# A decoder trunk on one core: the delta rule's input projections as nested block products

## The chip, the cores and the metric

The kernel runs on one core of a Trainium2 chip. The metric is the device time of one execution in microseconds (us). TensorE (PE) multiplies matrices and writes into the eight banks of PSUM; VectorE (DVE), ScalarE (ACT) and GpSimd (POOL) compute element by element; DMAs are issued here by SyncE (SP) and, a few, by POOL.

## What is computed

One layer over 1024 tokens of width 1024, all in float32. Cut to what matters:

```python
x = x + 0.5 * swiglu(rms_norm(x, ffn1_norm), gate1, up1, down1)    # width 2816
h = rms_norm(x, mix_norm)
proj = einsum("bld,de->ble", h, w_in)      # 8 delta-rule heads, 16 SSM heads, gates
q, k, v = split(silu(causal_dwconv(gdn_qkv, gdn_conv_w)))          # 4 taps, per channel
o = gated_delta_rule(q, k, v, g, beta)     # chunked recurrence, 8 heads of 128
o = rms_norm(o, gdn_norm_w) * silu(gdn_z)
y = ssd_scan(...)                          # Mamba-2 heads, gated and normalised
x = x + concat(o, y) @ w_out
x = x + 0.5 * swiglu(rms_norm(x, ffn2_norm), gate2, up2, down2)
return rms_norm(x, final_norm)
```

A delta-rule head needs four blocks of 128 columns of `w_in`: q, k, v and the output gate z (`COL_Q`, `COL_K`, `COL_V`, `COL_GZ`).

## The kernel before

**Matmuls in three.** Every large product is done on float32 operands split into a high part, rounded to the format that TensorE reads at full rate, and a low part, the remainder: high x high, high x low, low x high (`mm3`). A split is a cast on ACT and a subtraction on DVE (`wsplit` for weights, `split` elsewhere).

**Stages.** In order: the first gate and up projections (`gate_up_all`), the first down projection (`down_all`), four SSM units (`un`, four heads each), eight delta-rule heads (`h`), the out projection, and gate, up and down again. Gate, up and down are already done as 7 block products for 8: the operands are cut in 2 x 2 blocks, seven sums of blocks of each side are multiplied, and the results are combined. `prep(grp)` in `gate_up_all` makes the operands of the next product, `hid_store` writes the result to DRAM in the seven sums that the down projection reads. In the down projection `m3`, in the pool `dtmp0`, takes the first product's result (L596).

**A head.** `next_w()` gives two column blocks of `w_in`, split into `whi` and `wlo`, and loads the next ones. `proj_half` runs 8 x 3 matmuls for one block of 128 columns and one half of the tokens into a bank of the tag `pj` (three banks). `conv_silu` copies the two halves to `pre`, multiplies by the last tap, adds the other three taps with three DVE instructions over 1024 tokens (L784), and takes the silu. For z the silu goes straight from the bank (L1124). Then come the products `kt` x `kt` and `kt` x `qt` (L1149, L1150), the inverse of the 32 x 32 blocks by 31 steps of two small DVE instructions (`fx`, L1206 and L1208) with trips through DRAM (`fs_u`, `fs_x`), the merges to 128 x 128 on TensorE (L1226 to L1254), `kd` (L1265), and the recurrence over eight blocks of 128 tokens. A step of it is `kt` x state, `rr`, `u` x `rr`, `vn` (L1282), the output, and the new state `sn` (L1294).

**After the heads.** `out_start`, in the text of head 7, loads the first group of `w_out` and the SSM results into `wst`, splits them into `whi`, `wlo` and `mtt`; `group_tile` multiplies them. `nat` and `zg` are buffers of the out projection.

**Order.** The text is written stage by stage; the framework puts each engine's instructions, and each queue's DMAs, in an order of its own. It goes by readiness in its plan and prefers what stands earlier in the text, so that the projections of a later head fill TensorE between the steps of an earlier head's recurrence. On the chip each engine and each queue runs its list in that order, and each instruction waits by semaphores for its operands and for the release of the buffer that it writes. A pool opened where a closed one lay takes its memory, tile by tile.

Of the kernel before, what the change touches and what calls it, by code (L numbers as in the profile page):

```python
# [44 lines left out]
def kernel(  # L45
# [17 lines left out]
    def psum(tag):  # L63
        return ps.tile([P, 512], F32, name="ps_" + tag, tag=tag, bufs=PS_BUFS[tag])
# [8 lines left out]
    g_scr = dram.tile([NG, L], F32, name="g_scr")  # L73
    mix_scr = [dram.tile([P, NB, 256], F32, name=f"mix_scr{i}") for i in range(4)]
# [151 lines left out]
    def hsl(h, k, s):  # L226
        return h[k // 2][:, k % 2, s]
# [14 lines left out]
    def split(hi, lo, src):  # L242
        return split2(hi, lo, src)[1]
# [108 lines left out]
    def gate_up_all(pool, H, w_gate, w_up, scr, raws, ops, last, work, tail):  # L352
# [66 lines left out]
        for i, (p, w) in enumerate(todo):  # L419
# [209 lines left out]
    for h in range(GH):  # L629
        w_seq.append((COL_Q + h * P, COL_K + h * P))  # L630
        w_seq.append((COL_V + h * P, COL_GZ + h * P))
# [6 lines left out]
    def next_w():  # L638
        w = w_ready.pop(0)
        prefetch()  # L640
        return w

# [129 lines left out]

    def conv_silu(pool, w, j, cw, c, dst, bias=None, between=None):
# [9 lines left out]
        for t in range(3):  # L783
            V.scalar_tensor_tensor(out=dst, in0=pre[:, t:t + L], scalar=cw[:, t, c:c + 1], in1=dst,  # L784
                                   op0=ALU.mult, op1=ALU.add)
# [124 lines left out]

    rstd_g = []
    for un in range(4):
# [35 lines left out]
        proj_z(zts)  # L948
        xdts, xes = [], []
# [16 lines left out]
        def state():  # L966
# [3 lines left out]
            sn = s2p.tile([P, 256], F32, name="sn2", bufs=6)  # L970
# [135 lines left out]

    cn = ExitStack()
    natp = cn.enter_context(tc.tile_pool(name="natp", bufs=1, side="right", reuse_waits="tile"))
    with ExitStack() as cg:
        g1 = cg.enter_context(tc.tile_pool(name="gdn1", bufs=1, reuse_waits="tile"))  # L1110
        g2 = cg.enter_context(tc.tile_pool(name="gdn2", bufs=2, reuse_waits="tile"))
        for h in range(GH):
# [64 lines left out]
            qsq = g1.tile([P, L], F32, name="qsq")  # L1177
# [81 lines left out]
            for half in range(2):  # L1259
                pt = psum("sc")  # L1260
                for i in range(4):
                    b = half * 4 + i
                    T.transpose(pt[:, i * P:(i + 1) * P], kt[:, b * P:(b + 1) * P], ident)
                hb = slice(half * 4, half * 4 + 4)
                V.tensor_tensor(out=kd[:, hb], in0=pt.rearrange("p (i c) -> p i c", i=4),  # L1265
                                in1=wend[:, hb, h:h + 1].to_broadcast([P, 4, P]), op=ALU.mult)
# [3 lines left out]
            for b in range(NB):  # L1270
# [11 lines left out]
                V.tensor_scalar(out=vn, in0=p2[:, 0:P], scalar1=br2[:, b:b + 1], scalar2=None, op0=ALU.mult)  # L1282
# [204 lines left out]
```

## Time and profile before

| | us |
|---|---|
| median of 3 runs | 2309.29 (2308.17 to 2310.2) |
| the profiled execution | 2309.97 |
| its span in the trace | 2308.2 |
| PE busy | 2272.5 (98%) |
| DVE busy | 1725.1 (75%) |
| ACT busy | 1088.8 (47%) |
| POOL busy | 53.1 (2%) |
| DMA | 281.42 MB, mean 122 GB/s |

Busy time is the union of an engine's instructions. PE rows overlap (a matmul's printed duration is longer than its share of a run of matmuls), so distances between starts say more than durations. Issuing a DMA is not counted as busy. An idle time in a row is that of the engine just before these instructions, with what released it.

### The profile page before, as it was taken

To read this page: it belongs to the slowest core of one execution; us is meant where nothing else is said; L and a number is where in the kernel's file an instruction comes from. 1 tells how busy PE (TensorE), PEld (TensorE's weight loads), DVE (VectorE), ACT (ScalarE), POOL (GpSimd) and SP (SyncE) were. 2 spreads that over 40 slices of the span, in tenths; PEclk is the share of its full clock that TensorE was granted. 3 is DMA by queue.
4 is the path that set the end of the run, shared out by engine and by line. 5 is a ranking of instruction groups with operands and counts; after the bars stand their busy time and mean duration, and the time that the engine had idled before them with its cause. 6 is when DMAs were issued, how large, how long until landed. Compare 5 with 4: busy or idle time off the path is not lost.

```text
span 2308.2 us, 31393 instructions
## 1 busy us (share of the span) xinstructions
PE 2272.5 (98%) x11750; PEld 1858.9 (81%) x11750; DVE 1725.1 (75%) x3349; ACT 1088.8 (47%) x1884; POOL 53.1 (2%) x125
## 2 busy tenths in 40 slices
PE   7999999999999999999999999999999999999998
PEld 5788888888878888878788888788778888888886
DVE  7977776767765675668777888878688777766787
ACT  7433333343367785863555555332543333334344
POOL 0000000000000100000000000000000000000000
PEclk9999999999999999999999999999999999999999
DMA  3333332573652332232333322335223333329446
GB/s 111 127 114 102 105 109 97 178 278 128 222 179 78 92 92 81 67 85 74 83 101 83 82 74 73 104 110 193 79 84 117 109 103 105 109 88 354 139 154 214
DMA packets 231438, 281.42 MB, mean 122 GB/s; under 512 B 57449, under 2 KB 164045, under 8 KB 230261
## 3 DMA queue, kind: packets, MB, share of 16 engines
q1 hardware_dynamic: 231028, 279.31, 37.5%
q8 instruction: 92, 1.51, 0.3%
q14 instruction: 62, 0.50, 0.1%
q0 software_dynamic: 256, 0.10, 0.0%
HBM read 211.59 MB, written 67.77 MB: 121 GB/s over the span
## 4 chain that ended last, share of the span: by engine, by line
PE 87%; DVE 6%; ACT 3%; DMA 2%; issue 1%; SPq 0%; POOL 0%; DVEq 0%; ACTq 0%
PE ps_pj L121 9%; PE ps_pj L123 9%; PE ps_pj L122 9%; PE ps_pj L334 6%; PE ps_pj L332 6%; PE ps_pj L333 6%; PE ps_mx L332 3%; PE ps_mx L334 3%; PE ps_mx L333 3%; PE ps_pj L553 2%; PE ps_pj L554 2%; PE ps_pj L552 2%; PE ps_oo L333 2%; PE ps_oo L332 2%; PE ps_oo L334 2%; PE ps_sc L552 1%
## 5 line engine op out<-in xcount | busy, mean ns | idle before, releaser
L121 PE MATMUL ps_pj<-hhi,whi 128*128 128x512 f32 x832 | 334.3, 402 | 0.4 <-ACT gsb L826 0.4
L123 PE MATMUL ps_pj<-hhi,wlo 128*128 128x512 f32 x832 | 334.5, 402 | 0.0
L122 PE MATMUL ps_pj<-hlo,whi 128*128 128x512 f32 x832 | 331.8, 399 | 0.0
L334 PE MATMUL ps_pj<-bh,al 128*128 128x512 f32 x688 | 267.9, 389 | 0.0
L333 PE MATMUL ps_pj<-bl,ah 128*128 128x512 f32 x688 | 267.8, 389 | 0.0
L332 PE MATMUL ps_pj<-bh,ah 128*128 128x512 f32 x688 | 267.6, 390 | 0.0
L123 PEld LDWEIGHTS ps_pj<-hhi,wlo 128*128 128x128 f32 x832 | 156.7, 188 | 29.6 <-issue 1.9
L122 PEld LDWEIGHTS ps_pj<-hlo,whi 128*128 128x128 f32 x832 | 156.7, 188 | 29.1 <-issue 1.2
L121 PEld LDWEIGHTS ps_pj<-hhi,whi 128*128 128x128 f32 x832 | 156.8, 188 | 28.8 <-ACT gsb L826 0.9
L239 ACT CAST ah<-wst 128x512 fp32r<-128x512 f32 x88 | 54.6, 623 | 223.8 <-PE ps_oo L333 131.4
L239 ACT CAST hid<-hraw 128x1024 fp32r<-128x1024 f32 (+1 forms) x84 | 82.3, 981 | 147.9 <-PE ps_oo L554 62.5
L333 PEld LDWEIGHTS ps_pj<-bl,ah 128*128 128x128 f32 x688 | 129.2, 188 | 26.8
L334 PEld LDWEIGHTS ps_pj<-bh,al 128*128 128x128 f32 x688 | 129.1, 188 | 26.7
L332 PEld LDWEIGHTS ps_pj<-bh,ah 128*128 128x128 f32 x688 | 128.9, 188 | 26.5
L315 DVE TENSOR_TENSOR as<-wst 128x512 f32<-128x512 f32 x220 | 144.8, 683 | 3.3 <-DMA wst<-in_ffn_w_up_dram 3.1
L240 DVE TENSOR_TENSOR al<-as,ah 128x512 fp32r<-128x512 f32 x220 | 140.9, 684 | 4.8 <-ACT ah L239 4.0
L332 PE MATMUL ps_mx<-bh,ah 128*128 128x512 f32 x352 | 138.3, 395 | 4.0 <-ACT m L341 1.4
L333 PE MATMUL ps_mx<-bl,ah 128*128 128x512 f32 x352 | 138.3, 393 | 0.5 <-DVE bl L240 0.5
L334 PE MATMUL ps_mx<-bh,al 128*128 128x512 f32 x352 | 137.7, 391 | 0.3 <-DVE al L240 0.3
L239 ACT CAST ah<-as 128x512 fp32r<-128x512 f32 x220 | 125.0, 618 | 22.6 <-DVE as L315 22.6
L240 DVE TENSOR_TENSOR hid<-hraw,hid 128x1024 fp32r<-128x1024 f32 (+1 forms) x84 | 95.0, 1131 | 34.8 <-ACT hid L239 34.3
L341 ACT COPY m<-ps_pj 128x512 f32<-128x512 f32 x88 | 51.6, 588 | 124.5 <-PE ps_pj L334 122.3
(448 smaller groups left out, 5085.0 us busy)
## 6 DMA issues: line engine op xcount, KB each, us to landing
hraw<-hid_scr SPq DMA_DIRECT2D x70, 512.0 KB, 3.9
hid_scr<-hs SPq DMA_DIRECT2D x110, 256.0 KB, 2.3
wst<-in_ffn_w_down_dram SPq DMA_DIRECT2D x50, 512.0 KB, 4.7
wst<-in_ffn_w_gate_dram SPq DMA_DIRECT2D x22, 1024.0 KB, 5.6
wst<-in_ffn_w_up_dram SPq DMA_DIRECT2D x22, 1024.0 KB, 5.4
wst<-in_w_in_dram SPq DMA_DIRECT2D x36, 512.0 KB, 4.8
hid_scr<-sg SPq DMA_DIRECT2D x44, 256.0 KB, 2.0
keep<-in_ffn_w_down_dram SPq DMA_DIRECT2D x20, 512.0 KB, 5.5
```

What stands on the lines that cost most here:

```text
L121: T.matmul(o, lhsT=wh, rhs=mh, start=first, stop=False)
L122: T.matmul(o, lhsT=wh, rhs=ml, start=False, stop=False)
L123: T.matmul(o, lhsT=wl, rhs=mh, start=False, stop=last)
L239: return (A.copy(out=hi, in_=src), V.tensor_tensor(out=lo, in0=src, in1=hi.bitcast(F32), op=ALU.subtract))
L240: V.tensor_tensor(out=lo, in0=src, in1=hi.bitcast(F32), op=ALU.subtract))
L315: V.tensor_tensor(out=t, in0=v[0], in1=v[1], op=v[2])
L332: T.matmul(bank, lhsT=wh[:, k], rhs=bh[:, k], start=a, stop=False, skip_group_check=True)
L333: T.matmul(bank, lhsT=wh[:, k], rhs=bl[:, k], start=False, stop=False, skip_group_check=True)
L334: T.matmul(bank, lhsT=wl[:, k], rhs=bh[:, k], start=False, stop=z, skip_group_check=True)
L341: A.copy(out=t, in_=bank)
L552: T.matmul(bank, lhsT=hh, rhs=wh, start=first and k == 0, stop=False, skip_group_check=True)
L553: T.matmul(bank, lhsT=hh, rhs=wl, start=False, stop=False, skip_group_check=True)
```

## The change

The projections of heads 1 to 7 become block products too. For a pair of column blocks (q and k, or v and z: a *chunk*) the weights, 1024 x 256, are cut into a11, a12 (the first block's two halves of the input width) and a21, a22 (the second's); the tokens' operand into b11, b12 (first half of the width; first and second half of the tokens), b21, b22. Seven products of 512 x 128 by 512 x 512, with three matmuls per 128 rows each, take the place of eight.

- The weights' operands of all 14 chunks (a11, a12, a22 and four sums; high and low part) are made by `win_units`, a generator that `prep` advances during the first gate and up phase; what is left over is run behind that phase in the text. A unit's high part is an ACT copy; its low part is an ACT negation of the high part, to which a DMA issued by POOL adds the source; a second DMA from POOL stores both to DRAM (`wu_scr`). The pool `side0` holds a raw chunk (one buffer) and the units (two).
- The tokens' operands for products 7, 6, 5 and 4 are made in the four SSM units, one 128-row block each (`token_operands`), and stored (`t_scr`). After head 0 they are loaded into `nat` and `zg`, `whi` and `wlo`, and, for product 4, over a part of `hhi` and `hlo`.
- A head loads its 14 units through four slots in `wst`, four products ahead, and forms the results by adding in PSUM and with copies (`chunk`). The convolution reads them from SBUF in halves (`conv_from`).
- `kd` and `vn` move from DVE to ACT. `sn2` has 5 buffers for 6; `qsq` shares the buffer of `zc`.

Cut to its core:

```diff
+    IN_ORDER = (1, 6, 2, 7, 5, 3, 4)
+    def win_units(pool, tmp):
+        for c, scr in enumerate(wu_scr):
+            h = c // 2 + 1
+            raw = pool.tile([P, 2, NK, P], F32, name="wraw")
+            for j, c0 in enumerate(((COL_Q, COL_K), (COL_V, COL_GZ))[c % 2]):
+                nc.sync.dma_start(out=raw[:, j], in_=win_v[:, :, c0 + h * P:c0 + (h + 1) * P])
+            a11, a12, a21, a22 = raw[:, 0, 0:4], raw[:, 0, 4:8], raw[:, 1, 0:4], raw[:, 1, 4:8]
+            def unit(m, src):
+                u = pool.tile([P, 2, 4, P], F32R, name="wunit", bufs=2)
+                A.copy(out=u[:, 0], in_=src)
+                lo = u[:, 1].bitcast(F32)
+                A.mul(out=lo, in_=u[:, 0].bitcast(F32), mul=-1.0)
+                G.dma_start(out=lo, in_=src, accum_op=ALU.add)
+                G.dma_start(out=scr[:, IN_ORDER.index(m)].rearrange("p i (k c) -> p i k c", k=4),
+                                in_=u.bitcast(F32))
+            def summed(x, y, op):
+                t = tmp.tile([P, 4, P], F32, name="wsum", tag="m2f")
+                V.tensor_tensor(out=t, in0=x, in1=y, op=op)
+                return t
+            yield
+            unit(1, a11)
+            yield
+            unit(2, a12)
+            s1 = summed(a21, a22, ALU.add)
+            yield
...
@@ gate_up_all, prep
+                next(side, None)
@@ gate_up_phase
+            with tc.tile_pool(name=f"side{n}", bufs=1, reuse_waits="tile") as sp:
+                side = win_units(sp, npool) if n == 0 else iter(())
+                gate_up_all(npool, H, w_gate, w_up, hid_scr[n], raws, ops, last, work, [dn.prep, dn.prep], side)
+                for _ in side:
+                    pass
@@ SSM unit, behind proj_z(zts)
+        token_operands(un)
...
+    def unit_load(s):
+        if s < 7 * len(wu_scr):
+            c, i = divmod(s, 7)
+            u = slots[s % 4]
+            nc.sync.dma_start(out=u.bitcast(F32), in_=wu_scr[c][:, i])
+            units.append((s, u))
+    def unit_prod(bank, m, first):
+        s, u = units.pop(0)
+        bh, bl = H_IN[m]
+        for k in range(4):
+            wh, wl = (u[:, i, k * P:(k + 1) * P] for i in range(2))
+            T.matmul(bank, lhsT=wh, rhs=bh[k], start=first and k == 0, stop=False, skip_group_check=True)
+            T.matmul(bank, lhsT=wh, rhs=bl[k], start=False, stop=False, skip_group_check=True)
+            T.matmul(bank, lhsT=wl, rhs=bh[k], start=False, stop=k == 3, skip_group_check=True)
+        unit_load(s + 4)
+    def chunk(d0, d1):
+        lo, hi = slice(0, 512), slice(512, L)
+        x = psum("pj")
+        unit_prod(x, 1, True)
+        A.copy(out=d1[:, lo], in_=x)
+        y = psum("pj")
+        unit_prod(y, 6, True)
+        V.tensor_tensor(out=y, in0=y, in1=d1[:, lo], op=ALU.add)
+        A.copy(out=d0[:, hi], in_=y)
+        unit_prod(x, 2, False)
+        A.copy(out=d0[:, lo], in_=x)
+        unit_prod(y, 7, False)
+        z = psum("pj")
+        unit_prod(z, 5, True)
+        A.copy(out=d1[:, hi], in_=z)
+        V.tensor_tensor(out=d1[:, hi], in0=y, in1=d1[:, hi], op=ALU.add)
+        unit_prod(z, 3, False)
+        V.tensor_tensor(out=d0[:, hi], in0=z, in1=d0[:, hi], op=ALU.add)
+        unit_prod(y, 4, False)
+        A.copy(out=d1[:, lo], in_=y)
+    def conv_from(pre, c, dst):
+        for i in range(2):
+            ts = slice(i * 512, (i + 1) * 512)
+            A.mul(out=dst[:, ts], in_=pre[:, 3 + i * 512:3 + (i + 1) * 512], mul=cw_g[:, 3, c:c + 1])
+            for t in range(3):
+                V.scalar_tensor_tensor(out=dst[:, ts], in0=pre[:, t + i * 512:t + (i + 1) * 512],
+                                       scalar=cw_g[:, t, c:c + 1], in1=dst[:, ts], op0=ALU.mult, op1=ALU.add)
+        A.activation(out=dst, in_=dst, func=AF.Silu)
...
@@ heads
+            else:
+                pre = [gp.tile([P, 1028], F32, name="pre"), g1.tile([P, 1028], F32, name="pre2")]
...
+                chunk(pre[0][:, 3:3 + L], pre[1][:, 3:3 + L])
+                conv_from(pre[0], h, qt)
+                conv_from(pre[1], 8 + h, kt)
...
+                chunk(pre[:, 3:3 + L], zc)
+                conv_from(pre, 16 + h, vt_)
+                A.activation(out=zc, in_=zc, func=AF.Silu)
...
-                V.tensor_tensor(out=kd[:, hb], in0=pt.rearrange("p (i c) -> p i c", i=4),
-                                in1=wend[:, hb, h:h + 1].to_broadcast([P, 4, P]), op=ALU.mult)
+                for i in range(4):
+                    b = half * 4 + i
+                    A.mul(out=kd[:, b], in_=pt[:, i * P:(i + 1) * P], mul=wend[:, b, h:h + 1])
...
-                V.tensor_scalar(out=vn, in0=p2[:, 0:P], scalar1=br2[:, b:b + 1], scalar2=None, op0=ALU.mult)
+                A.mul(out=vn, in_=p2[:, 0:P], mul=br2[:, b:b + 1])
```

More of the change, by code (lines that the diff above doesn't have):

```diff
@@ L73 @@
     g_scr = dram.tile([NG, L], F32, name="g_scr")
+    wu_scr = [dram.tile([P, 7, 2, 512], F32, name=f"wu_scr{i}") for i in range(2 * GH - 2)]
+    t_scr = {m: dram.tile([P, 2, 4, 512], F32, name=f"t_scr{m}") for m in (4, 5, 6, 7)}
     mix_scr = [dram.tile([P, NB, 256], F32, name=f"mix_scr{i}") for i in range(4)]
@@ L628 @@
         w_seq.append((COL_SZ + un * 256, None))
-    for h in range(GH):
-        w_seq.append((COL_Q + h * P, COL_K + h * P))
-        w_seq.append((COL_V + h * P, COL_GZ + h * P))
+    w_seq.append((COL_Q, COL_K))
+    w_seq.append((COL_V, COL_GZ))
     w_ready = []
@@ L782, in conv_silu @@
             A.mul(out=dst[:, half * 512:(half + 1) * 512], in_=p, mul=cw[:, 3, c:c + 1])
-        for t in range(3):
-            V.scalar_tensor_tensor(out=dst, in0=pre[:, t:t + L], scalar=cw[:, t, c:c + 1], in1=dst,
-                                   op0=ALU.mult, op1=ALU.add)
+        conv_taps(pre, cw, c, dst)
         if bias is None:
@@ L909, in token_sums, with token_operands, put, step @@
         nc.sync.dma_start(out=dst, in_=scr.rearrange("j (c p) -> p (j c)", p=P))
+    def token_operands(k):
+        b11, b12, b21, b22 = ([hsl(t, k + 4 * i, slice(j * 512, (j + 1) * 512)).bitcast(F32) for t in (hhi, hlo)]
+                              for i in range(2) for j in range(2))
+        def put(m, t):
+            hi = tt.tile([P, 512], F32R, name="thi")
+            lo = tt.tile([P, 512], F32R, name="tlo")
+            split(hi, lo, t)
+            for i, part in enumerate((hi, lo)):
+                nc.sync.dma_start(out=t_scr[m][:, i, k], in_=part.bitcast(F32))
+        def step(t, x, y, op):
+            V.tensor_tensor(out=t, in0=x, in1=y, op=op)
+        t = tt.tile([P, 512], F32, name="tsum")
+        step(t, b22[0], b12[0], ALU.subtract)
+        step(t, t, b22[1], ALU.add)
+        step(t, t, b12[1], ALU.subtract)
+        put(7, t)
+        step(t, t, b11[0], ALU.add)
+        step(t, t, b11[1], ALU.add)
+        put(6, t)
+        step(t, b22[0], t, ALU.subtract)
+        step(t, t, b22[1], ALU.add)
+        put(5, t)
+        for x, y in ((b21[0], b22[0]), (b21[1], b22[1])):
+            step(t, t, y, ALU.subtract)
+            step(t, t, x, ALU.add)
+        put(4, t)
+    tt = cs_.enter_context(tc.tile_pool(name="tokens", bufs=1, side="right", reuse_waits="tile"))
     rstd_g = []
@@ new lines, in first_token_tiles @@
+    def first_token_tiles():
+        H_IN[7] = []
+        for i, tag in enumerate(("nat", "zg")):
+            t = natp.tile([P, 4, 512], F32R, name="t3", tag=tag)
+            nc.sync.dma_start(out=t.bitcast(F32), in_=t_scr[7][:, i])
+            H_IN[7].append([t[:, k] for k in range(4)])
+        for m in (6, 5):
+            H_IN[m] = []
+            for i, tag in enumerate(("whi", "wlo")):
+                t = wp.tile([P, 4, 512], F32R, name=f"t{m}", tag=tag)
+                nc.sync.dma_start(out=t.bitcast(F32), in_=t_scr[m][:, i])
+                H_IN[m].append([t[:, k] for k in range(4)])
+        for m, k0, j in ((1, 0, 0), (2, 4, 0), (3, 4, 1), (4, 0, 1)):
+            H_IN[m] = [[hsl(t, k0 + k, slice(j * 512, (j + 1) * 512)) for k in range(4)] for t in (hhi, hlo)]
+        for i, t in enumerate((hhi, hlo)):
+            for j in range(2):
+                nc.sync.dma_start(out=t[j][:, :, 512:L].bitcast(F32), in_=t_scr[4][:, i, 2 * j:2 * j + 2])
+        for i in range(2):
+            t = wp.tile([P, 2, 2, 512], F32R, name="wunits", tag="wst")
+            slots.extend(t[:, j] for j in range(2))
+        for s in range(4):
+            unit_load(s)
@@ L1107 @@
+    slots, H_IN = [], {}
     cn = ExitStack()
```

50 lines of the change are left out of this document (36 added, 14 removed).

## The prediction

> **What bounds the kernel now.** I read the page first (shares, chain, costliest groups), then busy time by stretch, then single stretches in order of time.
>
> ```profile
> span 2308.2 us, 31393 instructions
> PE 2272.5 (98%) x11750; PEld 1858.9 (81%) x11750; DVE 1725.1 (75%) x3349; ACT 1088.8 (47%) x1884; POOL 53.1 (2%) x125
> PE 87%; DVE 6%; ACT 3%; DMA 2%; issue 1%; SPq 0%; POOL 0%; DVEq 0%; ACTq 0%
> L121 PE MATMUL ps_pj<-hhi,whi 128*128 128x512 f32 x832 | 334.3, 402 | 0.4 <-ACT gsb L826 0.4
> ```
>
> TensorE is busy 98% of the span and carries 87% of the chain that ended last. The projections, L121 to L123, are its largest group, with no idle time before them worth the name. The kernel is bound by the number of matmuls it issues, as long as every other engine stays ahead. By stretch (us; then busy time and instructions of PE, PEld, DVE, ACT, POOL; clock, DMA share, GB/s): first gate and up phase, its beginning of the down phase, the SSM units, heads 0 to 6.
>
> ```profile
> 10.00:493.00 483.00, 475.34 (x2106) 389.30 (x2107) 371.76 (x598) 202.43 (x342) 0.00 (x0) 1.00 0.38 131
> 463.00:493.00 30.00, 30.00 (x133) 24.54 (x132) 18.11 (x18) 14.84 (x18) 0.00 (x0) 1.00 0.99 376
> 680.00:1008.00 328.00, 327.30 (x1877) 269.09 (x1876) 206.19 (x284) 243.81 (x446) 26.55 (x37) 1.00 0.29 86
> 1064.00:1437.00 373.00, 371.27 (x2543) 299.86 (x2541) 295.93 (x981) 194.37 (x391) 17.77 (x59) 1.00 0.30 78
> ...
> L1247 PE MATMUL ps_sc<-lv,u x128: 218/218/267, 1070.6 to 1518.8; 64*64 64x64 f32 x128
> ```
>
> In every stage PE leaves 1 to 2% idle. DVE and ACT have room everywhere, DVE least (0.77 to 0.79 in the first and the last of these stretches). The DMA engines are a third busy, except in one stretch where 376 GB/s is 0.99 of them: that is their ceiling here. L1247 runs once a head, so a head takes (1518.8 - 1070.6) / 7 = 64.0 us.
>
> A matmul's printed duration overlaps its neighbours. What one costs is the distance of starts in an undisturbed run:
>
> ```profile
> 1287.62 0.39 PE L121 MATMUL ps_pj<-hhi,whi 128*128 128x512 f32 x1
> ...
> 1302.12 0.39 PE L122 MATMUL ps_pj<-hlo,whi 128*128 128x512 f32 x1
> ```
>
> 64 steps lie between these two: 14.50 / 64 = 0.2266 us.
>
> **The change, part by part.** *1. Fewer matmuls.* Before, a head has 4 column blocks x 2 token halves x 8 k x 3 = 192 projection matmuls. After, it has 2 chunks x 7 products x 4 k x 3 = 168, of the same shape. Over 7 heads 168 go: 168 x 0.2266 = **-38.1 us**, on the path, since PE is the path.
>
> *2. DVE and ACT in a head.*
>
> ```profile
> L136 ACT CAST whi<-wst 128x1024 fp32r<-128x1024 f32 x64 | 65.9, 1048 | 41.7 <-PE ps_pj L122 27.7 <-PE ps_pj L123 9.5 <-DMA wst<-in_w_in_dram 4.5
> L137 DVE TENSOR_TENSOR wlo<-wst,whi 128x1024 fp32r<-128x1024 f32 x64 | 77.7, 1220 | 10.6 <-ACT whi L136 9.7
> L782 ACT ACTIVATE qt<-ps_pj,cols 128x512 f32<-128x512 f32 x16 | 11.1, 691 | 0.1
> L341 ACT COPY m<-ps_pj 128x512 f32<-128x512 f32 x88 | 51.6, 588 | 124.5 <-PE ps_pj L334 122.3 <-DVE as L315 1.2 <-ACT m L467 0.7
> L784 DVE SCALAR_TENSOR_TENSOR qt<-pre,cols,qt 128x1024 f32<-128x1024 f32 x24 | 30.7, 1280 | 6.8 <-ACT qt L782 6.6
> L461 DVE TENSOR_TENSOR m<-ps_pj,m 128x512 f32<-128x512 f32 x40 | 27.6, 690 | 4.0
> L1265 DVE TENSOR_TENSOR kd<-ps_sc,wend 128x512 f32<-128x512 f32 x16 | 10.9, 681 | 1.1 <-PE ps_sc L1263 0.7
> L1282 DVE TENSOR_SCALAR vn<-ps_sc,br 128x128 f32<-128x128 f32 x64 | 22.3, 348 | 9.4 <-PE ps_sc L1280 9.1
> L1137 ACT ACTIVATE dt<-dt,ngc 128x128 f32<-128x128 f32 x64 | 20.3, 393 | 0.1
> ```
>
> DVE loses 4 wlo, 2 kd and 8 vn (4.9 + 1.4 + 2.8 = 9.0 us). It gains 6 additions on banks (4.1) and 18 half-wide taps for 9 wide ones (18 x 0.69 against 9 x 1.28, +0.9): -4.0. ACT loses 4 whi, 6 copies, 6 multiplies and 2 silus (4 x 1.05 + 8 x 0.59 + 6 x 0.69 = 13.1). It gains 10 copies, 6 multiplies, a wide silu of two half ones' time (1.2), 8 kd and 8 vn (5.9 + 4.1 + 1.2 + 16 x 0.39 = 17.4): +4.3. At 64 us a head DVE had 50.8 and ACT 33.3. At 58.6 they have 46.8 and 37.6, so neither becomes the bound. A vn takes 0.39 for 0.35; but it now queues behind ACT's wide instructions (1.05) where it queued behind DVE's (1.28). I take nothing.
>
> *3. Waits on banks.* In a chunk the products alternate over three banks, and each copy or addition has another product (12 x 0.2266 = 2.7 us) to hide behind, but one: product 3 accumulates into z, and ACT must first have copied z after product 5. Uncovered, that is 14 x 0.59 = 8 us; the next chunk's first product and the previous head's recurrence are free to be put there. I take 2, bounds 0 and 8. A unit's load (512 KB, 4.8 us below) is issued as its slot empties and has three products, 8.2 us: hidden; without that cover it is 4.8 us a product.
>
> *4. Into the out projection.* The units hold both `wst` buffers, and the token operands `whi` and `wlo`, to the end of head 7.
>
> ```profile
> wst<-in_w_out_dram SPq DMA_DIRECT2D x8, 1024.0 KB, 5.1
> L1088 ACT ACTIVATE mtt<-nat,cols x8: 1137/1147/1152, 1433.4 to 1503.4; 128x1024 fp32r<-128x1024 f32 x8
> L121 PE MATMUL ps_pj<-whi,mtt x192: 387/389/504, 1435.3 to 1608.7; 128*128 128x512 f32 x192
> ```
>
> The first `mtt` matmul now comes at 1435.3, as the last projections end. After, the 1 MB in the second buffer can load only then: 5.1 + 1.15, and as much on DVE, are 7.5 us. Head 7's small products cover a part. +5, bounds 0 and 7.5.
>
> *5. Token operands.* Each SSM unit gets 15 DVE instructions of 512 columns (15 x 0.69 = 10.3 us), 4 ACT casts and 8 stores. DVE goes from 206 to 247 of 328 us, so this hides behind the projections that follow; but DVE is in order, and `xdt` stands behind it. +4, bounds 0 and 20 (half of each block uncovered).
>
> *6. The weight operands, in the gate and up phase.* 14 chunks of one 1 MB load, 7 units and 4 sums; a unit is an ACT copy, an ACT negation, an accumulating DMA (256 KB) and a store (512 KB), the last two issued by POOL.
>
> ```profile
> L315 DVE TENSOR_TENSOR as<-wst 128x512 f32<-128x512 f32 x220 | 144.8, 683 | 3.3 <-DMA wst<-in_ffn_w_up_dram 3.1
> L239 ACT CAST ah<-as 128x512 fp32r<-128x512 f32 x220 | 125.0, 618 | 22.6 <-DVE as L315 22.6
> hid_scr<-hs SPq DMA_DIRECT2D x110, 256.0 KB, 2.3
> x_scr<-xtb SPq DMA_DIRECT2D x8, 512.0 KB, 2.8
> wst<-in_w_in_dram SPq DMA_DIRECT2D x36, 512.0 KB, 4.8
> colst<-in_gdn_conv_w_dram POOLq DMA_DIRECT2D x1, 48.0 KB, 5.7
> colst<-in_ffn_norm_dram POOLq DMA_DIRECT2D x2, 4.0 KB, 6.4
> L596 ACT ACTIVATE m<-ps_pj x6: 584/589/598, 481.5 to 2117.8; 128x512 f32<-128x512 f32 x6
> ...
> L1066 SPq DMA_DIRECT2D zg<-z_scr x8: 319/384/578, 1008.4 to 1591.9; - x8
> ```
>
> DVE gets 56 x 0.68 = 38 us, ACT 98 x 1.24 = 122; both fit (410 and 324 of 483). The serial loop is what counts: two `wunit` buffers, one raw buffer. If both accumulations are issued ahead of the stores, two units take 1.24 + a + s, a and s being the times from issue to landing. With about 2.5 us a chunk until the next raw load is in, all is done at 12 + 35 + 98 x (1.24 + a + s) / 2. It has to be done when `m3`, which takes that memory, is written: 481.5 (L596). The program can run ahead of its text (L1066, text of the out projection, starts at 1008), so the start near 12 is open to it. This gives a + s = 7.6 us as the point from which it decides. No accumulating DMA is in the trace. The nearest in size, kind and load are the stores of 256 and 512 KB, a + s = 2.3 + 2.8 = 5.1: done at 358. The nearest from POOL, at the crowded start, give 5.7 + 6.4 = 12.1: done at 701. I take 6.8, nearer to the stores by size, for POOL's slower start: done at 441, **0 us**. Without the cover it is rival A.
>
> [...]
>
> **Sum.** -38.1 + 2 + 5 + 4 + 0 = -27. The profiled execution took 2309.97 (1.8 outside its span), 0.7 above the median, 2309.29; so 2283 either way.
>
> **Rivals.** *A, the other side: the loop of part 6 becomes the bound.* ACT and POOL are in order: a `wunit` copy that waits for a late store holds up the casts (L239) that feed PE. Beside the 131 GB/s of this stage, 14.7 MB of loads, 25.7 of accumulations and 51.4 of stores by 481.5 make 325 GB/s, against 376 at a share of 0.99; such a share lengthens every landing, and an accumulation also reads what it adds to. At a + s = 9 the loop ends at 549, 67 us late: 2283 + 67 = 2350; at 12.1, 220 late: 2503. From 7.6 on it costs, from 8.2 on it eats the 27. Against it: 5.1 from the stores.
>
> [...]
>
> *B, the change does not do what it says: a head stays at 64 us.* The recurrence of a head, the exponentials and products for the head after next, the small triangular solve on DVE and its trips through DRAM form a loop over two heads. The merges start some 2.3 us after the last row of the solve can have landed:
>
> ```profile
> lv<-fs_x SPq DMA_DIRECT2D x32, 32.0 KB, 1.9
> 1311.66 0.46 SPq L1218 DMA_DIRECT2D lv<-fs_x  x1
> 1315.92 0.21 PE L1226 MATMUL ps_sc<-lv,u 32*32 32x32 f32 x1
> ```
>
> If that loop binds, PE idles the 38 us instead, and parts 4 and 5 stay: 2309 - 0 to 8 (DVE's 4 us a head on that loop, in part) + 9 = 2310 to 2318. Against it: DVE is relieved, the wide instructions between the solve's steps are halved, and PE was never seen waiting there (1.7 us in 373).
>
> **How the numbers follow.** The forecast, 0.58, with its own range 2268 to 2300: from all covers holding (-38, and some 4 from a shorter loop) to half the bounds of parts 3 to 5. A 0.30: 2312 to 2503, most of it below 2350. B 0.12, three quarters of it within 0.2% (about what a measurement here tells from no change, 4.6 us). Faster 0.58, same 0.09, slower 0.33. The range for 8 in 10 goes from 2268 to 2345, leaving out A's far part.
>
> **What would show it.** PE matmuls 11582 for 11750, and a head at 58 to 60 us between L1247's groups, show part 1; 64 shows B. In the first phase: DMA share near 0.8 with PE still at 98%, and `m3` near 481, show part 6; PE idle released by ACT `ah`, ACT idle released by the stores of `wunit`, and a phase that ends later show A, and make the forecast wrong. PE idle ahead of the first `mtt` products sizes part 4, in front of `xdt` part 5.

## The result, and the profile after

The changed kernel takes 2524.64 us (median of 4 runs) where the kernel before takes 2309.56 in the same session: a ratio of 1.0936, 95% interval 1.0917 to 1.0955. It is 215 us slower; the forecast was 2283. Code lines of before stand 2 lines or more later after the change (L332 is L334, L341 is L343, L239 is L241, L552 is L555, L824 is L878, L1247 is L1428 and so on).

From the page after, as before: the span, the busy times, the mean granted clock and the DMA share in 40 slices, and the first line of the chain.

```profile
span 2521.6 us, 32207 instructions
PE 2314.4 (92%) x11582; PEld 1867.5 (74%) x11582; DVE 1772.4 (70%) x3462; ACT 1215.1 (48%) x2203; POOL 190.5 (8%) x321
PEclk9998988898789999999999999999999999999999
DMA  3677778789854734432655555543522332337545
PE 59%; issue 11%; DMA 10%; DVE 8%; ACT 5%; POOL 2%; POOLq 0%; SPq 0%; ACTq 0%; DVEq 0%
```

TensorE carried 87% of the chain and carries 59%. The damage is in the first third: there seven of the first twelve clock digits are below 9, and the DMA digits are mostly 7 to 9. By stretch (same columns as in the prediction):

```profile
10.00:493.00 483.00, 399.43 (x1629) 316.58 (x1629) 316.58 (x531) 226.26 (x405) 89.31 (x127) 0.91 0.71 206
493.00:600.00 107.00, 89.18 (x341) 70.10 (x342) 61.35 (x95) 45.71 (x79) 24.96 (x35) 0.89 0.84 249
600.00:725.00 125.00, 68.13 (x237) 52.08 (x236) 46.63 (x50) 47.13 (x68) 23.89 (x34) 0.74 0.84 261
725.00:880.00 155.00, 152.57 (x689) 125.69 (x688) 112.49 (x145) 67.95 (x89) 0.65 (x2) 1.00 0.54 177
1216.00:1641.00 425.00, 409.48 (x2676) 324.95 (x2675) 324.33 (x1170) 218.46 (x506) 18.80 (x62) 0.98 0.57 169
1641.00:1660.00 19.00, 13.18 (x61) 10.11 (x60) 17.16 (x62) 11.61 (x14) 1.04 (x6) 0.73 0.63 176
```

The first row had 475 us of TensorE and a clock of 1.00 before. No engine is full in it, not even the DMA engines (0.71). So something waits. The waits of the whole trace (engine, tile, line, then who ended the wait: us, times, longest), and the stores of the units (first and last start):

```profile
ACT wunit L659 <- DMA wu_scr<-wunit: 280.3, 66, 10.8
POOL wu_scr L663 <- DMA wunit<-wsum: 189.7, 48, 8.6
POOL wu_scr L663 <- DMA wunit<-wraw: 109.1, 34, 8.3
PE ps_pj L334 <- ACT m L343: 81.3, 20, 10.6
PE ps_pj L555 <- ACT m L599: 22.6, 1, 22.6
L663 POOL DMA_DIRECT2D wu_scr<-wunit x98: 547/552/880, 75.7 to 725.4; - x98
wu_scr<-wunit POOLq DMA_DIRECT2D x98, 512.0 KB, 3.9
wunit<-wsum POOLq DMA_DIRECT2D x56, 256.0 KB, 4.8
wunit<-wraw POOLq DMA_DIRECT2D x42, 256.0 KB, 4.2
```

98 units take 650 us, 6.7 each, and the first store is issued at 75.7: the first raw load is issued at 65.5 us. POOL waits for each accumulation to land before it issues the store; ACT waits for that store before it may write the buffer again; behind ACT's copy stand the copies that empty TensorE's banks (L343) and the casts of its operands (L241). The row of L599 is `m3`, which takes the units' memory: it is written at 719.8 us for 481.5 before, and TensorE waits 22.6 us for it in the down phase. ACT's timeline shows the first kind of wait (start, duration; the idle time before it, and its end, in brackets):

```profile
302.50 0.59 ACT L343 COPY m<-ps_pj 128x512 f32<-128x512 f32 x1
308.95 0.62 ACT L659 CAST wunit<-wsum 128x512 fp32r<-128x512 f32 x1 [5.86 <-DMA wu_scr<-wunit]
309.60 0.63 ACT L661 ACTIVATE wunit<-wunit 128x512 f32<-128x512 f32 x1
310.14 0.60 ACT L241 CAST ah<-wst 128x512 fp32r<-128x512 f32 x1
...
318.16 0.62 ACT L659 CAST wunit<-wraw 128x512 fp32r<-128x512 f32 x1 [3.73 <-DMA wu_scr<-wunit]
...
319.86 1.13 ACT L241 CAST ah<-as 128x512 fp32r<-128x512 f32 x2
328.29 0.62 ACT L659 CAST wunit<-wsum 128x512 fp32r<-128x512 f32 x1 [7.29 <-DMA wu_scr<-wunit]
328.94 0.63 ACT L661 ACTIVATE wunit<-wunit 128x512 f32<-128x512 f32 x1
329.47 0.57 ACT L343 COPY m<-ps_pj 128x512 f32<-128x512 f32 x1
```

The copies at 302.5 and 329.5 empty TensorE's banks; between them ACT stands three times, 5.9, 3.7 and 7.3 us, for a store that TensorE has no use for yet. Four markers cut the span into stages (first gate-weight matmul; first multiplication by the last tap in head 0, L838; last projection matmul; first `mtt` matmul):

```profile
L878 PE MATMUL ps_pj<-hhi,gw x16: 387/395/478, 878.6 to 895.7; 128*64 128x512 f32 x16
L1210 PE MATMUL ps_pj<-hhi,wunits x224: 387/393/501, 1215.9 to 1640.9; 128*128 128x512 f32 x112
L123 PE MATMUL ps_pj<-whi,mtt x192: 387/389/796, 1654.2 to 1824.3; 128*128 128x512 f32 x192
```

| stage (us) | before | after | one-chunk kernel (below) |
|---|---|---|---|
| gate, up, down | 667.5 | 878.6 (+211.1) | 669.0 |
| SSM units | 287.4 | 289.7 (+2.3) | 289.8 |
| projections of the heads | 479.4 | 473.0 (-6.4) | 471.7 |
| to the first `mtt` product | 1.0 | 12.9 (+11.9) | 12.8 |
| the rest | 872.9 | 867.4 (-5.5) | 868.8 |

Two questions follow: how the 211 come about, and where some 32 of the 38 us of saved matmuls went (38.1 less the 6.4 in the table).

### The profile page after: what moved, and what is told of

The parts are those of the page before. It is cut to its first block, busy times and chain, and to the rows that moved or that the text cites. A ratio compares the mean times of both kernels' runs of the same rounds, so it can differ in the third digit from the quotient of the medians.

```text
span 2521.6 us, 32207 instructions
## 1 busy us (share of the span) xinstructions
PE 2314.4 (92%) x11582; PEld 1867.5 (74%) x11582; DVE 1772.4 (70%) x3462; ACT 1215.1 (48%) x2203; POOL 190.5 (8%) x321
## 4 chain that ended last, share of the span: by engine, by line
PE 59%; issue 11%; DMA 10%; DVE 8%; ACT 5%; POOL 2%; POOLq 0%; SPq 0%; ACTq 0%; DVEq 0%
DMA wu_scr<-wunit 5%; PE ps_pj L123 5%; PE ps_pj L124 5%; PE ps_pj L125 5%; PE ps_pj L334 3%; PE ps_pj L336 3%; PE ps_pj L335 3%; PE ps_pj L1210 2%; PE ps_pj L1211 2%; PE ps_pj L1212 2%; DMA wunit<-wsum 2%; PE ps_pj L556 2%; PE ps_pj L555 2%; PE ps_pj L557 2%; POOL wunit L662 2%
## 5 line engine op out<-in xcount | busy, mean ns | idle before, releaser
L334 PE MATMUL ps_pj<-bh,ah 128*128 128x512 f32 x688 | 283.2, 413 | 82.0 <-ACT m L343 81.3
L335 PE MATMUL ps_pj<-bl,ah 128*128 128x512 f32 x688 | 280.7, 408 | 0.0
L336 PE MATMUL ps_pj<-bh,al 128*128 128x512 f32 x688 | 280.2, 407 | 0.0
L334 PEld LDWEIGHTS ps_pj<-bh,ah 128*128 128x128 f32 x688 | 135.9, 198 | 119.2 <-ACT m L343 90.0
L336 PEld LDWEIGHTS ps_pj<-bh,al 128*128 128x128 f32 x688 | 136.8, 199 | 30.7 <-DVE al L242 0.8
L125 PE MATMUL ps_pj<-hhi,wlo 128*128 128x512 f32 x384 | 152.9, 398 | 0.0
L123 PE MATMUL ps_pj<-hhi,whi 128*128 128x512 f32 x384 | 152.2, 396 | 0.4 <-ACT gsb L880 0.4
L124 PE MATMUL ps_pj<-hlo,whi 128*128 128x512 f32 x384 | 151.4, 394 | 0.0
L334 PE MATMUL ps_mx<-bh,ah 128*128 128x512 f32 x352 | 139.8, 399 | 10.5 <-ACT m L343 5.9
L555 PE MATMUL ps_pj<-wd,hid 128*128 128x512 f32 x264 | 106.2, 405 | 40.5 <-ACT m L599 22.6
L241 ACT CAST hid<-hraw 128x1024 fp32r<-128x1024 f32 (+1 forms) x84 | 82.1, 978 | 126.4 <-PE ps_oo L557 57.1
L241 ACT CAST ah<-as 128x512 fp32r<-128x512 f32 x220 | 125.5, 618 | 21.5 <-DVE as L317 21.5
L242 DVE TENSOR_TENSOR al<-wst,ah 128x512 fp32r<-128x512 f32 x88 | 60.5, 688 | 93.2 <-ACT ah L241 93.0
L659 ACT CAST wunit<-wsum 128x512 fp32r<-128x512 f32 x56 | 34.7, 620 | 173.2 <-DMA wu_scr<-wunit 150.9
L241 ACT CAST ah<-wst 128x512 fp32r<-128x512 f32 x88 | 54.1, 617 | 129.3 <-PE ps_oo L335 72.6
L556 PE MATMUL ps_pj<-wd,hid 128*128 128x512 f32 x264 | 106.7, 404 | 2.8 <-DVE wd L242 2.7
```

The lines of the kernel that those rows point to most:

```text
L123: T.matmul(o, lhsT=wh, rhs=mh, start=first, stop=False)
L124: T.matmul(o, lhsT=wh, rhs=ml, start=False, stop=False)
L125: T.matmul(o, lhsT=wl, rhs=mh, start=False, stop=last)
L241: return (A.copy(out=hi, in_=src), V.tensor_tensor(out=lo, in0=src, in1=hi.bitcast(F32), op=ALU.subtract))
L242: V.tensor_tensor(out=lo, in0=src, in1=hi.bitcast(F32), op=ALU.subtract))
L334: T.matmul(bank, lhsT=wh[:, k], rhs=bh[:, k], start=a, stop=False, skip_group_check=True)
```

## Experiments: the gate and up phase

Runs without an interval have one time each. The times of one kernel spread by up to 0.5% (2308.78 to 2320.88 us in one of the runs below), so differences of up to some 12 us between single runs say little.

**One chunk.**

```diff
-        for c, scr in enumerate(wu_scr):
+        for c, scr in enumerate(wu_scr[:1]):
-            nc.sync.dma_start(out=u.bitcast(F32), in_=wu_scr[c][:, i])
+            nc.sync.dma_start(out=u.bitcast(F32), in_=wu_scr[0][:, i])
```

> Left out: the weight operands of 13 of the 14 chunks; all heads read those of the first chunk. Theory A (the preparation of the operands in the gate and up phase carries the loss): the two first stages, 211 us longer after the change, come back to within 15 us of before, the first gate-weights matmul at 668 to 683 for 878.6, and the time is 2313 to 2330. Rival (the changed heads and the narrower margins of the whole kernel carry a good part of it): the time stays above 2380. In either case theory B (the recurrence of a head binds) keeps a head at 63 to 64 us between the groups of L1428, and the time at or above before; if the transfers of the preparation were what slowed the heads, a head comes to 58 to 60 and the time to 2285 or less.

2315.91 us, ratio 1.0023 (1.0013 to 1.0033). The first stages are back (669.0), so the preparation costs about 209 of the 215. But the kernel that gets its operands for nearly nothing is still not faster than before: the second question stands by itself.

**Stores from SP; POOL's subtraction; both.**

```diff
-                A.mul(out=lo, in_=u[:, 0].bitcast(F32), mul=-1.0)
-                G.dma_start(out=lo, in_=src, accum_op=ALU.add)
+                G.tensor_tensor(out=lo, in0=src, in1=u[:, 0].bitcast(F32), op=ALU.subtract)   # POOL's subtraction, and both
-                G.dma_start(out=scr[:, IN_ORDER.index(m)]...
+                nc.sync.dma_start(out=scr[:, IN_ORDER.index(m)]...                            # stores from SP, and both
```

> The stores of the units are issued by SP instead of POOL; the accumulating DMAs stay with POOL. Theory 'order on POOL' (POOL waits for a landing before each store, so that one unit is in flight): with two units in flight they take (1.24 + 4.5 + 3.9) / 2 = 4.8 us each for 6.7, the last is done near 70 + 98 x 4.8 = 540 for 725, and 120 to 170 us come back: 2355 to 2405. Rival 'bandwidth' (the landings are long because the DMA engines are shared by too much at a time): the rate stays 6 to 6.7 us a unit, 2470 to 2525. Rival 'SP's queue': the loads of the weights now stand behind stores that wait, and PE idles by DMA wst: slower than 2525.

> The low part of a unit is a POOL subtraction instead of an ACT negation and an accumulating DMA; the stores stay with POOL. Theory 'accumulating DMA' (its landing is the larger part of the serial chain): a unit is a copy of 0.62, a subtraction of about 1 (an estimate from POOL's 1.4 to 1.7 us for twice the columns) and a store of 3.9; the loop takes 2.8 to 5.5 us a unit, is done between 350 and 610, and 100 to 211 us come back: 2313 to 2425. Rival 'the stores' (their 51 MB and their landings alone fill the loop): 6 us a unit and more, above 2470.

> Both edits: the low part by a POOL subtraction, the stores issued by SP. Theory 'one unit in flight': the loop is 2.5 to 3 us a unit, done before 400, and the first two stages are as before within 15 us: 2313 to 2330. Rival 'bandwidth': 51 MB of stores and 14.7 of loads beside the 131 GB/s of this stage make 267 GB/s by 481.5, below the 376 seen before; if landings still stretch, the stage ends 30 to 100 us later than before, 2340 to 2410. Rival 'SP's queue': PE idles by DMA wst, and it is slower than with the stores on POOL.

2478.45, 2391.35 and 2361.64 us. POOL's order alone is worth 46 us: with the stores on SP a unit still takes 6.3 us, not the 4.8 expected, as ACT goes on waiting for stores (179 us up to 860). The first and the last run missed their theories and came out in the ranges of "bandwidth"; a test of the bytes follows below. Without the accumulating DMAs the last store is issued at 479 us (494 with both edits) for 725, and 133 and 163 us come back. But the first stages still end 46 us later than in the one-chunk kernel. A part of that is a price of POOL's subtraction itself. DVE's addition `as`, in the one-chunk kernel and beside POOL's subtraction, and that subtraction:

```profile
L317 DVE TENSOR_TENSOR as<-wst 128x512 f32<-128x512 f32 x220 | 144.7, 683 | 2.0 <-DMA wst<-in_ffn_w_up_dram 1.9
```

```profile
L317 DVE TENSOR_TENSOR as<-wst 128x512 f32<-128x512 f32 x220 | 163.0, 771 | 2.3 <-DMA wst<-in_ffn_w_up_dram 2.2
L661 POOL TENSOR_TENSOR wunit<-wsum,wunit 128x512 f32<-128x512 f32 x56 | 98.2, 1759 | 187.8 <-ACT wunit L659 178.2 <-DVE al L242 9.6
```

**All of it on POOL.** Cast and subtraction on POOL (first run), the sums too (second).

```diff
-                A.copy(out=u[:, 0], in_=src)
+                G.tensor_copy(u[:, 0], src)          # and the subtraction on POOL, as above
-                V.tensor_tensor(out=t, in0=x, in1=y, op=op)      # the sums, second run only
+                G.tensor_tensor(out=t, in0=x, in1=y, op=op)
```

> The change with the unit's cast and subtraction both on POOL and the store issued by POOL; ACT does nothing for the units, the sums stay on DVE, the stored bytes are the same. Theory 'in-order ACT' (the 46 us that the kernel with POOL's subtraction and SP's stores still lost are ACT's copies that wait for a buffer, with PE's casts and copies behind them): the first stages come within 12 us of before, 2316 to 2330. Rival 'bandwidth': the stores still stretch everything, 2345 to 2400. Rival 'POOL is too slow or slows DVE' (1.5 to 1.8 us an instruction, DVE 0.90 for 0.69 beside it): the last unit later than 481, or DVE the bound; 2335 to 2400.

> As the kernel with the units on POOL, the four sums of a chunk on POOL too, so that neither ACT nor DVE waits for a buffer of the preparation. POOL has 98 x (3.1 to 3.5) + 56 x 1.6 + 98 x 0.56 = 448 to 490 us of work: by theory 'in-order engines' the last unit comes at 480 to 520 and the time is 2316 to 2345; by 'bandwidth' 2345 to 2400.

2418.32 and 2461.21 us, above every range; nearest is the rival "POOL slows DVE". ACT does nothing for the units any more; DVE has become late instead. TensorE's longest waits of the two runs up to the end of the down phase:

```profile
PE ps_pj L336 <- DVE al L242: 65.5, 12, 12.1
```

```profile
PE ps_pj L336 <- DVE al L242: 91.0, 10, 13.0
```

In the first, DVE's sums wait for POOL (50.5 us); in the second `as` takes 0.884 us, and DVE is idle 87 us ahead of it, for late loads of the weights (`wst`). So the theory "in-order ACT" is not enough: with the units off ACT, the wait stands in DVE's list, which carries TensorE's operands too; and with the sums off DVE as well, slower DVE instructions and late weights take its place. What made the weights late is not shown.

**Bytes or waits; the accumulation; DVE's subtraction.**

```diff
-                                in_=u.bitcast(F32))
+                                in_=raw[:, 0].rearrange("p (i k) c -> p i k c", i=2))    # stores read the raw chunk
-                G.dma_start(out=lo, in_=src, accum_op=ALU.add)
+                G.dma_start(out=lo, in_=src)                                             # plain copy
-                A.mul(...); G.dma_start(..., accum_op=ALU.add)
+                V.tensor_tensor(out=lo, in0=src, in1=u[:, 0].bitcast(F32), op=ALU.subtract)   # and stores from SP
```

> The store of a unit reads the raw chunk instead of the unit (the stored values are left wrong), so the bytes stay and a unit's buffer no longer waits for its store, nor a store for the accumulation. Theory 'wait' (ACT's next copy stands behind the store of its buffer, and PE's operands behind ACT): the loop is bounded by (1.24 + 0.86 + 4.5) / 2 = 3.3 us a unit for 6.7, PE's waits for ACT in the phase fall from 70 to below 25, and the time to 2330 to 2410. Theory 'bytes': the same DMA work at 0.7 to 0.9 of the engines, 2470 to 2525.

> The DMA that adds the source to the negated high part is a plain copy of the same 256 KB (the low part is left wrong). If accumulating is what makes these DMAs slow (it has to read what it adds to): they land in 3 us or less for 4.2 to 4.8, one unit is shorter by 1.2 to 1.8 us, and the time is 2350 to 2420. If it is the path from POOL and the load on the engines: 4 us and more still, 2490 to 2525.

> The low part by a DVE subtraction, no negation, no accumulating DMA, stores issued by SP, nothing on POOL. DVE gets 98 x 0.68 = 67 us: 372.8 + 38 + 67 = 478 of 483 in the first phase. Theory 'POOL's tensor work slows DVE beside it': as and al are back at 0.68 us (0.73 to 0.88 in the runs with POOL's subtraction), and the time is at or below that of the run with POOL's subtraction and SP's stores, 2335 to 2362. Rival 'DVE full': 478 of 483 with waits for ACT in between makes DVE the bound, 2365 to 2420.

2411.45, 2454.38 and 2392.62 us. The first is the clearest: the same bytes in less time, a DMA share of 0.86 for 0.71, landings that got *longer*, and 113 us gained:

```profile
10.00:493.00 483.00, 427.79 (x1795) 342.13 (x1796) 345.54 (x579) 262.88 (x468) 121.26 (x171) 0.95 0.86 252
wu_scr<-wraw POOLq DMA_DIRECT2D x98, 512.0 KB, 6.7
wunit<-wsum POOLq DMA_DIRECT2D x56, 256.0 KB, 5.5
```

So half of the 215 are not a matter of bytes: they come from what stands behind a store of a unit's buffer. The time is just above the range of "wait", and a unit takes 4.8 us where 3.3 were expected: ACT now waits for the accumulations instead (115 us up to 860), and TensorE's waits for L343 up to 500 us fell only from 69.9 to 51.2 ("below 25" missed). The plain copy lands in 3.5 to 3.8 us for 4.2 to 4.8: an accumulation is 0.7 to 1.0 us dearer, and 70 us come from it, for the last store is issued 69 us earlier (656). Both of its ranges missed: it is not as dear as the first one took it. With DVE's subtraction `as` is back at 0.682 beside an idle POOL, and the time is in the range of the rival "DVE full": DVE is 425 of 483 us busy by 493, and the rest of the units runs into the down phase.

**Subtractions shared, halves apart.**

```diff
+                E = V if m in (3, 5, 6, 7) else G
+                E.tensor_tensor(out=lo, in0=src, in1=u[:, 0].bitcast(F32), op=ALU.subtract)
+                # second run: high and low half are tiles of their own, each stored by itself
```

> Low parts of the four units with sums or of product 5 (3, 5, 6, 7) on DVE, of the other three on POOL; stores from SP. DVE gets 56 x 0.68 = 38 us instead of 67 or of POOL's slowing (0.77 to 0.80 for 0.68 over some 600 instructions, 55 us). If DVE's time in the phase is what is left, the time lies below both kernels with one kind of subtraction: 2335 to 2358. If ACT's waits for a buffer are, it stays at 2358 to 2375.

> As the run before it, and the high and low halves of a unit are buffers of their own, each stored by its own 256 KB DMA; the high half is stored as soon as ACT has written it. If ACT's copies waiting for a store are what is left, 10 us or more below the run before it; if SP's queue (196 stores for 98, each waiting in order ahead of the weights' loads) is, slower than it.

2371.70 and 2374.89 us: between the two pure versions, and no help from smaller buffers. In the second run ACT's waits for stores fell from 99 to 38 us (up to 860), and the time did not follow. So they are not what is left there. DVE is 437 of 483 us busy in it; whether that is what is left, no run here separates. No version with the full preparation came near 2309; the best gives back 163 of the 209 us.

## Experiments: the heads

**Is it the solve, or ACT's new work?** (Each on the one-chunk kernel; half the solve also on the kernel before.)

```diff
-            for j in range(31):
+            for j in range(16):                                   # half the solve
-                        A.mul(out=kd[:, b], ...); A.mul(out=vn, ...)
+                        V.tensor_tensor(out=kd[:, hb], ...); V.tensor_scalar(out=vn, ...)
```

> On top of the one-chunk kernel (2315.9 us, a head at 63.1): the inverse of the 32 x 32 blocks does 16 of its 31 steps; the last 15 are left out. By the rows of the one-chunk kernel a step is 0.219 + 0.212 us on DVE, so 6.5 us go from each head's solve. Theory B (a head is bound by a loop through DVE and the solve, TensorE follows): a head comes to 58 to 60 us and the time to 2280 to 2297. Rival 'queueing on ACT' or 'DMA': the head stays at 62 to 63, 2308 to 2316.

> The kernel before with the same 15 steps left out. If TensorE binds its heads (98% busy), nothing is gained but a part of its short waits: a head 63.5 to 64, 2304 to 2310. If the heads before stood at the same loop by chance (64.0 and 63.1 are near each other), they come down as well, by 2 us a head or more: below 2297.

> One-chunk kernel with kd and vn back on DVE, as before the change. Theory B (DVE's share of the loop binds): 4.2 us a head go back to DVE, the head goes up by 1 to 4 us: 2323 to 2345. Rival 'vn queues behind ACT's wide instructions, and this is what holds the recurrence': the head comes down by 1 us or more, 2308 or less. Within 4 us of 2316: neither.

2315.27 (ratio to before 1.0023, 1.0014 to 1.0033), 2312.10 (1.0012, 1.0002 to 1.0021) and 2317.61 us (1.0039, 1.0024 to 1.0053). 6.5 us less in each solve change nothing in either kernel, so theory B in the form "the solve is in a loop that binds" falls. `kd` and `vn` on ACT cost nothing, nor do they help.

**Fewer matmuls and nothing else.** The kernel before, less 168 projection matmuls.

```diff
         for k in range(NK):
+            if hd and k in (1, 2, 3):       # heads 1 to 7: high x high and high x low only
```

> The kernel before, with 24 of the 192 projection matmuls of each of heads 1 to 7 left out (low x high for three of eight k in each of 8 half blocks), 168 in all: the number that the change removes, without block products, loads or a changed order of the text. If a head follows the matmuls that TensorE has to do (the step of the prediction), 38 us go: 2268 to 2280, a head at 58 to 60. If a head is held near 64 us by the recurrence whatever the projections take (rival B), 2300 to 2312, with PE idle or thinly used in the heads.

2279.51 us, ratio 0.9868 (0.9853 to 0.9883). 168 matmuls are worth 30.3 us, 0.18 each, at 0.2266 apart. The projections end at 1401.7 for 1434.3, and the projections of heads 2 to 6 take 59.0 to 59.5 us each (63.3 to 64.2 before). The recurrences come down with them, to 57 to 60 us a head for the first five; the last two take 69 and 71, beside the out projection.

**The unit loads: none, from POOL, thin.**

```diff
-            nc.sync.dma_start(out=u.bitcast(F32), in_=wu_scr[0][:, i])
+            if s < 4: nc.sync.dma_start(...)                                    # none
+            G.dma_start(out=u.bitcast(F32), in_=wu_scr[0][:, i])                # from POOL
+            n = 512 if s < 4 else 32
+            nc.sync.dma_start(out=u[:, :, 0:n]..., in_=wu_scr[0][:, i, :, 0:n])  # thin
```

> One-chunk kernel in which only the first four unit loads are made; the other 94 are left out and the products read what lies there. The DMA share in the heads falls from 0.57 towards 0.35. Rival 'the loads lengthen the solve's trips through DRAM, and the loop with them': a head comes down by 2 us or more, 2300 or less. Theory B as DVE's loop: the head stays within 0.7 us of 63.1, 2311 to 2318.

> One-chunk kernel (2315.9 us); the 98 unit loads are issued by POOL instead of SP, so the bytes and their times are the same, but SP's queue holds only what it held before the change. Theory 'SP's queue' (loads that wait for their slot on SP hold up the small transfers of the solve behind them, and the reverse): the time comes to that of the kernel without unit loads, 2294 to 2304. Rival 'shared DMA engines' (share 0.57 for 0.23 lengthens every landing): it stays at 2311 to 2320. Rival 'POOL': memsets and masks of the heads stand behind loads that wait, slower than 2320.

> One-chunk kernel; after the first four, a unit load moves 32 of 512 columns (the products read old values elsewhere): slots, waits and the number of DMAs stay, 15/16 of the bytes go, and the DMA share in the heads goes from 0.57 to about 0.25. Theory 'bytes': the time comes to that of the kernel without loads, 2294 to 2303. Theory 'waits and order': it stays at 2308 to 2318.

2297.95 (0.9950, 0.9936 to 0.9965), 2313.95 (1.0020, 1.0008 to 1.0033) and 2303.49 us (0.9975, 0.9965 to 0.9985). Not SP's queue, then: from POOL nothing is gained, and the time is in the range of the rival "shared DMA engines". Without loads 18 us come back, with 1/16 of the bytes 12, half a microsecond above the range of "bytes". Yet the units themselves land in time. From POOL, where the trace has it, a load lands in 4.0 us (median) of the 12 between its issue and its use, and in the heads TensorE waited for one five times:

```profile
wunits<-wu_scr POOLq DMA_DIRECT2D x98, 512.0 KB, 4.0
PE ps_pj L1210 <- DMA wunits<-wu_scr: 6.6, 5, 2.1
```

The starts of every 168th projection matmul show where the time goes (us from head to head, heads 1 to 7):

| kernel | 1 | 2 | 3 | 4 | 5 | 6 | 7 |
|---|---|---|---|---|---|---|---|
| after | 53.7 | 59.6 | 61.0 | 65.7 | 60.0 | 66.0 | 59.4 |
| one chunk | 53.7 | 59.6 | 61.0 | 64.5 | 60.0 | 65.8 | 59.4 |
| thin loads | 46.4 | 60.3 | 59.8 | 60.9 | 59.3 | 59.4 | 59.2 |
| no loads | 46.1 | 59.1 | 59.6 | 61.5 | 59.5 | 59.4 | 59.4 |
| loads from POOL | 46.8 | 60.3 | 63.7 | 62.2 | 66.9 | 63.6 | 60.6 |

Most heads do take 59 to 61. Three places hold some 17 of the 20 us by which the one-chunk kernel lies above no loads: the second chunk of head 1, and the merges of the solves that fall into heads 4 and 6. In head 1 of the changed kernel (ACT, DVE and TensorE together, in order of time):

```profile
1246.71 1.06 ACT L1245 ACTIVATE kt<-kt 128x1024 f32<-128x1024 f32 x1 [1.78 <-DVE kt L1243]
1247.68 0.57 ACT L1220 COPY zc<-ps_pj 128x512 f32<-128x512 f32 x1
1248.30 0.50 PE L1210 MATMUL ps_pj<-hhi,wunits 128*128 128x512 f32 x1 [1.68 <-ACT zc L1220]
1253.24 0.69 DVE L1223 TENSOR_TENSOR ps_pj<-ps_pj,zc 128x512 f32<-128x512 f32 x1
1253.97 0.58 ACT L1224 COPY pre<-ps_pj 128x512 f32<-128x512 f32 x1 [5.72 <-DVE ps_pj L1223]
1254.61 0.80 PE L1210 MATMUL ps_pj<-t,wunits 128*128 128x512 f32 x1 [3.29 <-ACT pre L1224]
```

No load ends these two waits. The copy of the first product (L1220) stands in ACT's list behind a silu that waits for DVE's taps. The addition (L1223) has its operand at 1248.3, but stands in DVE's list behind 22 small steps of the solve. With thin loads, and with all the bytes loaded from POOL, one such step stands there, TensorE does not wait at these two places, and head 1 takes 46 to 47 us. So here it is the order of the lists, and not the bytes. TensorE's timeline at the merge in head 4 of the changed kernel:

```profile
1406.75 0.40 PE L1210 MATMUL ps_pj<-t,wunits 128*128 128x512 f32 x1
...
1409.18 1.11 PE L1428 MATMUL ps_sc<-lv,u 64*64 64x64 f32 x16 [0.57 <-ACT lv L1421]
1411.24 1.97 PE L1433 MATMUL ps_sc<-u,lv 64*64 64x64 f32 x16 [0.95 <-ACT u L1423]
1413.14 1.11 PE L1444 MATMUL ps_sc<-ident,kt 128*128 128x128 f32 x4
1413.90 0.78 PE L1210 MATMUL ps_pj<-t,wunits 128*128 128x512 f32 x1
```

No projection stands between the merges, small matmuls wait for ACT, and then the granted clock is 0.50 (from 1411 to 1415 us): sixteen small matmuls span 1.97 us at L1433, 1.14 where the clock holds, and the projections that follow start 0.43 us apart for 0.2266. For the merges the cause stays open between two. The lists are other ones when the loads are thin or gone, since they are written before the run by a plan that has the loads in it. But the solve's own transfers land later too: those of 32 KB take 3.2 to 3.8 us (medians) with the loads from POOL, and 1.7 to 2.7 with thin or no loads; that run loses its time in heads 3 to 6. No run here keeps the lists and takes away the bytes.

## Why the prediction was wrong, step by step

- **Part 6, "0 us": the step that failed.** It put three things too low. The start: it took 12 us, "open to it", and the first raw load is issued at 65.5. The landings: it took a + s = 6.8, and they came to 4.2 to 4.8 and 3.9, so a + s is 8.1 to 8.7. By the formula that is 504 to 534, and with the late start 557 to 587, some 75 to 105 us late, and not yet 725. The rest is the form of the loop, for it took both accumulations to be issued ahead of the stores. POOL's list mostly has accumulation, wait, store (58 of the 98 units; the other 40 go in pairs); a unit costs 6.7 us where the formula has 5.0 to 5.3 with its waits for raw loads. Also, the loop isn't free-running: its copies stand in ACT's list between TensorE's operands, so each side waits for the other. Rival A had named this wait (a `wunit` copy that holds up the casts) and gave 2312 to 2503, "most of it below 2350"; it came out at 2525. Its chance was too small, for its own break-even lay 0.8 us from the value that was taken.
- **A term that no part had: the clock.** Summed over the distances of starts up to the gate weights, TensorE's idle time went from 7 to 160 us, and matmuls at the half rate (0.43 us apart) cost 49 us for 3. These 153 and 45 are 198 of the 211. The prediction priced a wait at its length; here a wait costs nearly a third more.
- **Part 1, "-38.1": right in kind.** The pure test gives 30.3. In this kernel 6.4 of it are seen in the heads.
- **Part 3, +2 (0 to 8): 6.1 us of waits on banks, for another reason.** 1.1 of them are at product 3, the one that the part left uncovered. The other 5.0 are in head 1, where "each copy or addition has another product to hide behind" fails: that holds only if ACT and DVE start it at once, and there a copy starts some 4 us and an addition 5 us after its operands are there, behind other work in the same lists. Matmuls at the half rate behind these waits cost 2 to 3 us more. "A unit's load is hidden" is right of its landing; no part had a loss at the merges, and its cause is open (above).
- **Part 2, nothing:** right (2317.61 with `kd` and `vn` on DVE against 2315.91, the intervals overlap). **Part 5, +4:** 2.3.
- **Part 4, +5:** 11.9, beyond its bound of 7.5. The last product starts at 1641.3, but the load of `nat` is issued by SP at 1645.2, behind four stores of the solve (L1392, 1641.5 to 1644.1) and `z_scr`, which waited for ACT's silu: 3.9 us. From there to the first `mtt` product it is 9.0. So it is `nat`, which holds a token operand to the end of head 7, and not the second buffer of `wst` that the part named. The prediction had not counted the queue that this load is in, nor the lower clock (0.73 in that stretch).
- **Rival B** named 2310 to 2318 for heads that stay at 64 us, and the one-chunk kernel gives 2315.9 with the recurrences 63.1 us apart. The agreement is chance: with the same recurrence the kernel before ran 30 us faster on fewer matmuls.

Of the signs that the prediction listed, the waits of ACT for the stores of `wunit`, and of PE for ACT, point to A, rightly. "64 shows B" misleads: the groups of L1428 are 63.3 us apart in the changed kernel, and B's loop was not the cause.

## What to carry to other kernels

Work that only fills gaps must not stand in the in-order list of an engine that feeds the bound one, unless each of its waits is sure to be over: one late buffer there is paid by everyone behind it, and here moving the work to another engine mostly moved the wait. The same holds the other way round: a short copy that TensorE needs is late when it stands behind long work in its list. Price such a loop with the order it can fall into at worst, one item in flight, and if the break-even lies within the uncertainty of one landing time, take the loop as the likelier bound. And measure the pure gain first: the kernel before with the matmuls simply left out would have shown 30 us to be had, against 98 units at 6.7 us each to pay for them.

## What the runs showed of the hardware

- TensorE's granted clock fell to 0.50 behind some of its waits and stayed there for some microseconds. In head 1 of the one-chunk kernel an idle time of 3.30 us is followed by matmuls 0.43 us apart for 3.2 us, where 0.23 is the distance before and behind; at the same place of the changed kernel 3.29 us of idle time are followed by 5.7 us at a clock of 0.50. Behind the wait of 1.68 us a little ahead of it (1248.3 in the rows above) the clock is 1.00 and the matmuls stay 0.23 us apart. In the merge above two waits of 0.57 and 0.95 us among small matmuls went ahead of a clock of 0.50. So the length of the last wait does not tell by itself whether the clock falls: 1.68 us left it whole, 0.95 did not. What does is not shown here.
- DVE's additions took longer in the kernels in which POOL computes beside them: `as` takes 0.682 us (mean over the whole run) in the changed kernel and with DVE's subtraction, and 0.731 to 0.884 in the four kernels in which POOL makes all the subtractions. POOL needed 1.42 to 1.78 us for a subtraction in these four, and DVE 0.69 for the same one. In the same four kernels additions of two SBUF tiles (`m` from `m` and `m`, L449) took 0.723 to 0.951 us, for 0.689 in the changed kernel, and additions of a bank and an SBUF tile (L464) 0.683 or 0.684 in all five. How the two engines hinder each other, and how much of L464 ran beside POOL's work, is not shown.
- An accumulating DMA of 256 KB within SBUF lands 0.7 to 1.0 us later than a plain one of the same size (medians 4.2 and 4.8 us for 3.5 and 3.8; the shortest 3.2 for 2.2), at a DMA share of 0.71 and 0.66 up to 493 us.
